# Memory attention's softmax: two scalings moved from VectorE to ScalarE, and wider spacing of its steps in a hybrid decoder step

## The chip, the cores and the metric

One core of one Trainium2 chip runs the whole program. The metric is the device time of one execution in microseconds (us); a kernel is run three times or more and the median is compared.

## The reference

One layer of a decoder trunk is computed for 1024 prompt tokens and 8 single-token samples, with a model width of 1024. From the normalised input one projection gives the operands of three branches: a stick-breaking attention (8 heads of 64, over the prompt, and over a paged cache of 2048 tokens for the samples), a short convolution, and a softmax cross-attention of 4 heads of 128 into 256 memory tokens. The branches are projected, gated and summed, and a feed-forward block of 4096 follows. The change lies in the cross-attention of the prompt:

```python
def cross_attn(q, mk, mv):
    s = jnp.einsum('bqhd,bmhd->bhqm', q.astype(jnp.float32), mk.astype(jnp.float32)) * (1.0 / math.sqrt(XA_HEAD_DIM))
    p = jax.nn.softmax(s, axis=-1)
    o = jnp.einsum('bhqm,bmhd->bqhd', p, mv.astype(jnp.float32)).astype(mv.dtype)
    return o.reshape(q.shape[0], q.shape[1], XA_WIDTH)
...
q, k, v, cb, cc, ch, xq = split_in(xn @ w_in[l])
y_sb = sb_prompt(q, k, v, b_sb[l])
...
y_xa = cross_attn(xq, mk, mv)
xp = merge_and_ffn(xp, xn, y_sb, y_conv, y_xa, *tail)
```

## The kernel before

Nearly all products are done in three matmuls (`mm3`, lines 149 to 152): each fp32 operand is split into a high and a low part, and high-high, high-low and low-high are added up in PSUM. The weights come in by DMA on the SP queue, ScalarE casts the high part (`wh`, line 126) and VectorE subtracts for the low part (`wl`, line 129). The stages follow each other: norms and memory keys and values; then one long stage in which the gemms of the input projection and of the gates run on TensorE (tile `g`, outputs of 128 channels by the chunks 384, 384 and 264 tokens) while three small jobs are woven in between them; then the merge, the output projection and the feed-forward block, which are dense matmuls.

The order of TensorE's instructions is fixed by the program's own planner, the class `Stream` (lines 165 to 236): it keeps a clock `S_.t`, adds the estimated cost of each matmul to it, and takes a step of a woven-in job when that clock passes the step's due time. Each job is a generator; `yield 7700.0` means "continue 7.7 us later by that clock", and `yield "f"` means "when the PSUM buffers `f` are free to use, at least 2.2 us after the last user". VectorE, ScalarE and the DMA queues execute in an order that the tile scheduler builds ahead of time; each engine works strictly through its own list, so an instruction that waits holds all that stand behind it. Steps under `high()` are placed early in that list, steps under `low()` fill the rest.

The three jobs are:

- `attention()` (line 666): the stick-breaking attention of the prompt. For each head pair and block of 128 queries: scores (tile `z`), a chain of ScalarE and VectorE passes that ends in `m` (lines 644 to 659), transposes into `wt` (line 709), a copy `th` (line 713) and the product `av` (line 727).
- `xattn()` (line 777): the memory attention, 4 heads by 4 blocks of 256 queries, 16 rounds. A round has three steps on TensorE, each `XA_NS` after the one before: the six score matmuls (`f<-mk,xq`), then four transposes of the weights (`f<-ident,pr`, line 811), then the six matmuls with the values (`f<-xth,mv` and `xtl`). Between the first and the second step stands the softmax: VectorE takes the maximum `mx` (line 799) and scales it (line 800), ScalarE does two exponentials with their sums (line 802), VectorE takes the reciprocal `sm` (line 804) and scales the weights `pr` (line 805).
- `decode()` (line 928): the samples. Pages of the key cache are multiplied and summed on VectorE (`kv` and `z` or `xs`, lines 937 and 938, low priority), and later pages of the value cache go through TensorE (line 891).

The softmax and the number that spaces the three steps:

```python
nc.vector.tensor_reduce(out=mx, in_=sc, axis=AX.X, op=ALU.max)
nc.vector.tensor_scalar(out=mx, in0=mx, scalar1=-XSC, scalar2=None, op0=ALU.mult)
...
nc.vector.reciprocal(out=sm, in_=sm)
nc.vector.tensor_tensor(out=pr, in0=pr, in1=sm.unsqueeze(2).to_broadcast([P, 2, 256]), op=ALU.mult)
yield XA_NS
yield "f"
...
XA_NS = 7700.0
```

Of the kernel before, what the change touches and what calls it, by code (L numbers as in the profile page):

```python
# [12 lines left out]
AF = mybir.ActivationFunctionType  # L13
ALU = mybir.AluOpType
# [4 lines left out]
P = 128  # L19
# [12 lines left out]
XSC = 128.0 ** -0.5  # L32
# [4 lines left out]
def body(ctx, tc, I, O):  # L37
    nc = tc.nc
# [85 lines left out]
    def split(hi, lo, src, scale=None, eng=None):  # L124
        if scale is None:
            cast = nc.scalar.copy(out=hi, in_=src)  # L126
            if first_exp:
                behind(cast, first_exp.pop())
            (eng or nc.vector).tensor_tensor(out=lo, in0=src, in1=hi.bitcast(F32), op=ALU.subtract)  # L129
        else:  # L130
            nc.scalar.mul(out=hi, in_=src, mul=scale)
            nc.vector.scalar_tensor_tensor(out=lo, in0=src, scalar=scale, in1=hi.bitcast(F32),
                                           op0=ALU.mult, op1=ALU.subtract)
# [15 lines left out]
    def mm3(ps, lh, ll, rh, rl, first, last):  # L149
        nc.tensor.matmul(out=ps, lhsT=lh, rhs=rh, start=first, stop=False)  # L150
        nc.tensor.matmul(out=ps, lhsT=lh, rhs=rl, start=False, stop=False)  # L151
        nc.tensor.matmul(out=ps, lhsT=ll, rhs=rh, start=False, stop=last)  # L152
# [87 lines left out]
    def cost(n):  # L240
        return 3 * n / 2.4
# [19 lines left out]
    def high():  # L261
        return tc.high_priority(offset=HIGH)
# [514 lines left out]
    def xattn():  # L777
        for h in range(4):
            yield f"x{h}p"
            yield 5000  # L780
            mk = cp.tile([P, 2, NMEM], F32R, name="mk", bufs=1)
            mv = cp.tile([P, 2, 2, P], F32R, name="mv", bufs=1)
            nc.sync.dma_start(out=mk.bitcast(F32), in_=mkscr[h])
            nc.sync.dma_start(out=mv.bitcast(F32), in_=mvscr[h])
            for q0 in range(0, S, 256):
                xq = cp.tile([P, 2, 256], F32R, name="xq", bufs=1)
                nc.sync.dma_start(out=xq.bitcast(F32), in_=xqs[h][:, :, q0:q0 + 256])
                yield XA_NS
                yield "f"
                sc = pf.tile([P, 2, 256], F32, name="f")  # L790
                for j in range(2):
                    qs = slice(j * P, (j + 1) * P)
                    mm3(sc[:, j], xq[:, 0, qs], xq[:, 1, qs], mk[:, 0], mk[:, 1], True, True)
                    S_.t += cost(256)
                mx = cp.tile([P, 2], F32, name="mx")
                sm = cp.tile([P, 2], F32, name="sm")
                pr = cp.tile([P, 2, 256], F32, name="pr", bufs=1)
                with high():
                    nc.vector.tensor_reduce(out=mx, in_=sc, axis=AX.X, op=ALU.max)
                    nc.vector.tensor_scalar(out=mx, in0=mx, scalar1=-XSC, scalar2=None, op0=ALU.mult)  # L800
                    for j in range(2):
                        nc.scalar.activation(out=pr[:, j], in_=sc[:, j], func=AF.Exp, scale=XSC, bias=mx[:, j:j + 1],
                                             accum_out=sm[:, j:j + 1])
                    nc.vector.reciprocal(out=sm, in_=sm)
                    nc.vector.tensor_tensor(out=pr, in0=pr, in1=sm.unsqueeze(2).to_broadcast([P, 2, 256]), op=ALU.mult)
                yield XA_NS
                yield "f"
                pt = pf.tile([P, 2, 256], F32, name="f")
                for t in range(2):
                    for j in range(2):  # L810
                        nc.tensor.transpose(out=pt[:, t, j * P:(j + 1) * P], in_=pr[:, j, t * P:(t + 1) * P],
                                            identity=ident)
                        S_.t += 109
                th = wk.tile([P, 2, 256], F32R, name="xth", tag="th", bufs=4)
                tl = wk.tile([P, 2, 256], F32R, name="xtl", tag="tl", bufs=1)
                with high():
                    split(th, tl, pt)
                yield XA_NS
                yield "f"
                av = pf.tile([P, 512], F32, name="f")[:, :256]  # L820
                for t in range(2):
                    mm3(av, mv[:, 0, t], mv[:, 1, t], th[:, t], tl[:, t], t == 0, t == 1)
                    S_.t += cost(256)
                yo = cp.tile([P, 256], F32, name="yo", bufs=1)
                with high():
                    nc.scalar.copy(out=yo, in_=av)
                nc.scalar.dma_start(out=yscr[8 + h][:, q0:q0 + 256], in_=yo)
        S_.done.add("xa")

    XA_NS = 7700.0  # L830


    z4 = z.rearrange("p g (b h) -> p g b h", h=8)
# [242 lines left out]
    for u in "qqqqkvkxxxxkvkcgcgcgcgcgcgcgcgcgcgcgcggggggggggggg":  # L1076
        n = count[u] = count.get(u, -1) + 1
        dict(q=add_q, k=add_k, v=add_v, x=add_x, c=add_c, g=add_g)[u](n)
    S_.spawn(attention())
    S_.spawn(xattn())  # L1080
    S_.spawn(decode())
    S_.run(lambda: {"att", "xa", "c32", "late3"} <= S_.done)
# [386 lines left out]
```

## Time and profile before

| | us |
|---|---|
| median of 3 runs | 1930.6 (1930.37 to 1934.13) |
| the profiled execution, its own time | 1933.35 |
| span of the profiled execution | 1931.5 |
| TensorE matmul busy in the span | 1845.9 |
| VectorE busy | 1115.0 |
| ScalarE busy | 801.2 |

The profile is of one execution. Its span runs from the first instruction to the last; 1.85 us of its own time lie outside. In the rows, PE is TensorE, DVE is VectorE, ACT is ScalarE, and SP issues DMAs. A row of a timeline has the start in us, the duration, the engine, the line and the operation, and in square brackets the idle time ahead of the instruction with what ended it. A stretch in a table of windows gives the busy time of each engine in it and the TensorE clock that was granted, 1.00 for the higher of its two levels (2.4 GHz) and 0.50 for the lower (1.2 GHz).

### The profile page before, as it was taken

How to read it: one execution, taken by the hardware profiler on the slowest of the kernel's cores; microseconds unless marked ns; L12 is line 12 of the kernel's file. 1: busy time of each engine (PE TensorE's matmuls, PEld its weight loads, DVE VectorE, ACT ScalarE, POOL GpSimd, SP SyncE). 2: the span in 40 equal slices, each digit the busy share in tenths (PEclk: the TensorE clock that was granted, in tenths of full speed). 3: DMA queues.
4: the chain of work that ended last, by engine and by line, in shares of the span. 5: the costliest groups of instructions: out<-in, count | busy, mean ns of one | idle time of the engine just before them, and what ended most of it. 6: DMA issues, size and time to landing. Idle time of an engine off the chain costs nothing.

```text
span 1931.5 us, 31789 instructions
## 1 busy us (share of the span) xinstructions
PE 1845.9 (96%) x12226; PEld 1734.4 (90%) x12226; DVE 1115.0 (58%) x1910; ACT 801.2 (41%) x1641; POOL 48.7 (3%) x54
## 2 busy tenths in 40 slices
PE   6999888999799999999999999999999999999996
PEld 5998777889788778778999999999999999999996
DVE  5337987899956555542347457254555555554437
ACT  6324555656666656652334445422211111222223
POOL 1000000000000000000031000000000000000003
PEclk9999999999899999999999999999999999999998
DMA  7558665555623556667554422211111111111122
GB/s 255 151 164 254 204 186 180 171 176 182 211 86 104 159 171 198 204 206 247 186 181 154 131 94 83 77 44 55 44 55 45 44 44 44 45 44 55 44 88 88
DMA packets 219464, 249.14 MB, mean 129 GB/s; under 512 B 14488, under 2 KB 162672, under 8 KB 219312
## 3 DMA queue, kind: packets, MB, share of 16 engines
q1 hardware_dynamic: 204080, 230.17, 38.1%
q10 hardware_dynamic: 15008, 16.90, 2.5%
q8 instruction: 96, 1.57, 0.3%
q14 instruction: 56, 0.46, 0.1%
q0 software_dynamic: 224, 0.04, 0.0%
HBM read 201.67 MB, written 45.40 MB: 128 GB/s over the span
## 4 chain that ended last, share of the span: by engine, by line
PE 82%; DVE 9%; DMA 3%; ACT 3%; issue 3%; SPq 0%; DVEq 0%; ACTq 0%
PE g L150 9%; PE g L152 8%; PE g L151 8%; PE u L150 8%; PE u L151 8%; PE u L152 8%; PE w L150 6%; PE w L151 6%; PE w L152 6%; PE m L150 2%; PE m L151 2%; PE m L152 2%; PE av L727 2%; PE z L628 2%; PE f L891 1%
## 5 line engine op out<-in xcount | busy, mean ns | idle before, releaser
L150 PE MATMUL g<-xh,wh 128*128 128x384 f32 (+1 forms) x1152 | 388.0, 337 | 3.8 <-DVE ql L129 3.8
L152 PE MATMUL g<-xh,wl 128*128 128x384 f32 (+1 forms) x1152 | 370.4, 321 | 1.9 <-DVE wl L129 1.9
L151 PE MATMUL g<-xl,wh 128*128 128x384 f32 (+1 forms) x1152 | 369.8, 321 | 0.0
L1347 DVE TENSOR_TENSOR facc<-w,facc 128x384 f32<-128x384 f32 (+3 forms) x336 | 171.5, 514 | 143.3 <-PE w L152 143.3
L150 PEld LDWEIGHTS g<-xh,wh 128*128 128x128 f32 x1152 | 220.6, 191 | 33.2 <-issue 26.9
L150 PE MATMUL w<-fh,dh 128*128 128x384 f32 (+3 forms) x720 | 232.6, 323 | 3.0 <-ACT facc L1345 2.5
L151 PE MATMUL w<-fl,dh 128*128 128x384 f32 (+3 forms) x720 | 231.3, 321 | 0.0
L152 PE MATMUL w<-fh,dl 128*128 128x384 f32 (+3 forms) x720 | 230.7, 320 | 0.0
L150 PE MATMUL u<-xh,wh 128*128 128x384 f32 (+1 forms) x720 | 229.3, 318 | 0.0
L152 PE MATMUL u<-xh,wl 128*128 128x384 f32 (+1 forms) x720 | 228.5, 317 | 0.0
L151 PE MATMUL u<-xl,wh 128*128 128x384 f32 (+1 forms) x720 | 228.4, 317 | 0.0
L152 PEld LDWEIGHTS g<-xh,wl 128*128 128x128 f32 x1152 | 219.6, 191 | 2.1 <-DVE wl L129 2.1
L151 PEld LDWEIGHTS g<-xl,wh 128*128 128x128 f32 x1152 | 220.6, 191 | 0.0
L129 DVE TENSOR_TENSOR wl<-wr,wh 128x1024 fp32r<-128x1024 f32 x104 | 127.3, 1224 | 115.7 <-ACT wh L126 115.4
L126 ACT CAST wh<-wr 128x1024 fp32r<-128x1024 f32 x104 | 109.0, 1048 | 106.7 <-PE g L151 44.9
L150 PEld LDWEIGHTS w<-fh,dh 128*128 128x128 f32 x720 | 136.5, 190 | 5.0 <-ACT facc L1345 2.8
L126 ACT CAST dh<-wr 128x1024 fp32r<-128x1024 f32 x32 | 33.5, 1050 | 256.4 <-PE w L151 239.6
L152 PEld LDWEIGHTS w<-fh,dl 128*128 128x128 f32 x720 | 136.4, 189 | 0.7
L151 PEld LDWEIGHTS w<-fl,dh 128*128 128x128 f32 x720 | 136.5, 190 | 0.6
L151 PEld LDWEIGHTS u<-xl,wh 128*128 128x128 f32 x720 | 135.4, 188 | 0.0
L150 PEld LDWEIGHTS u<-xh,wh 128*128 128x128 f32 x720 | 135.3, 188 | 0.0
L152 PEld LDWEIGHTS u<-xh,wl 128*128 128x128 f32 x720 | 135.2, 188 | 0.0
(293 smaller groups left out, 3393.0 us busy)
## 6 DMA issues: line engine op xcount, KB each, us to landing
kv<-in_cache_k_pages SPq DMA_DIRECT2D x128, 256.0 KB
kv<-in_cache_v_pages SPq DMA_DIRECT2D x96, 256.0 KB
wr<-in_w_up SPq DMA_DIRECT2D x32, 512.0 KB
wr<-in_w_down SPq DMA_DIRECT2D x32, 512.0 KB
wr<-in_w_in SPq DMA_DIRECT2D x28, 512.0 KB
lg<-lgscr SPq DMA_DIRECT2D x24, 516.0 KB
wr<-in_w_gate SPq DMA_DIRECT2D x24, 512.0 KB
lgscr<-lg ACTq DMA_DIRECT2D x48, 192.0 KB
```

The source lines that it names most:

```text
L126: cast = nc.scalar.copy(out=hi, in_=src)
L129: (eng or nc.vector).tensor_tensor(out=lo, in0=src, in1=hi.bitcast(F32), op=ALU.subtract)
L150: nc.tensor.matmul(out=ps, lhsT=lh, rhs=rh, start=first, stop=False)
L151: nc.tensor.matmul(out=ps, lhsT=lh, rhs=rl, start=False, stop=False)
L152: nc.tensor.matmul(out=ps, lhsT=ll, rhs=rh, start=False, stop=last)
L628: nc.tensor.matmul(out=zt[:, :w_], lhsT=hq[es], rhs=hk[es, k0:k1], start=True, stop=half != 0, tile_position=(64 * e, 0))
L727: nc.tensor.matmul(out=av[0][es], lhsT=hv[:, j, es], rhs=th[:, i, e], tile_position=(0, 64 * e), start=(r + n == R and k == 0), stop=(r == ...
L891: nc.tensor.matmul(out=ps[32 * j:32 * j + 32], lhsT=w[:, g, 32 * i:32 * i + 32], rhs=ts[j // 2][:, j % 2], start=True, stop=True, tile_pos ...
L1347: nc.vector.tensor_tensor(out=facc[:, n, cs], in0=ps, in1=facc[:, n, cs], op=ALU.add)
```

## The change

Three edits, all in `xattn()`. The scaling of the maximum by a constant goes to ScalarE. The scaling of the weights by the reciprocal sum goes to ScalarE, as two instructions of 256 columns where there was one of 512. The spacing of a round's three steps goes from 7.7 to 9.4 us of the planner's clock.

```diff
                     nc.vector.tensor_reduce(out=mx, in_=sc, axis=AX.X, op=ALU.max)
-                    nc.vector.tensor_scalar(out=mx, in0=mx, scalar1=-XSC, scalar2=None, op0=ALU.mult)
+                    nc.scalar.mul(out=mx, in_=mx, mul=-XSC)
                     for j in range(2):
                         nc.scalar.activation(out=pr[:, j], in_=sc[:, j], func=AF.Exp, scale=XSC, bias=mx[:, j:j + 1],
                                              accum_out=sm[:, j:j + 1])
                     nc.vector.reciprocal(out=sm, in_=sm)
-                    nc.vector.tensor_tensor(out=pr, in0=pr, in1=sm.unsqueeze(2).to_broadcast([P, 2, 256]), op=ALU.mult)
+                    for j in range(2):
+                        nc.scalar.activation(out=pr[:, j], in_=pr[:, j], func=AF.Copy, scale=sm[:, j:j + 1])
                 yield XA_NS
...
-    XA_NS = 7700.0
+    XA_NS = 9400.0
```

The number of matmuls stays as it is; 48 steps of the memory attention move later among them, and the scheduler builds the lists of the other engines anew. Lines behind 805 are one higher after the change.

VectorE's list in round 3 of the memory attention, before: from the scaling of the maximum (`mx`) to the scaling of the weights (`pr`). `kv` and `z` are the decode's page products, `u`, `a` and `m` the stick-breaking attention's.

```order
L800 TENSOR_SCALAR mx<-mx 128x2
L649 SCALAR_TENSOR_TENSOR u<-u,a 128x384
L651 TENSOR_TENSOR u<-m,u 128x384
L937 TENSOR_TENSOR kv<-kv,qb 128x1024
L651 TENSOR_TENSOR u<-m,u 128x384
L652 SCALAR_TENSOR_TENSOR a<-u,cy,a 128x384
L804 RECIPROCAL sm<-sm 128x2
L937 TENSOR_TENSOR kv<-kv,qb 128x1024
L938 TENSOR_REDUCE z<-kv 128x2x8
L652 SCALAR_TENSOR_TENSOR a<-u,cy,a 128x384
L658 TENSOR_TENSOR m<-m,a 128x384
L805 TENSOR_TENSOR pr<-pr,sm 128x512
```

The same place now: from the maximum to the reciprocal, which is VectorE's last part in the softmax.

```order
L799 TENSOR_REDUCE mx<-f 128x2
L939 TENSOR_REDUCE z<-kv 128x2x8
L129 TENSOR_TENSOR wl<-wr,wh 128x1024
L658 TENSOR_TENSOR m<-m,a 128x384
L938 TENSOR_TENSOR kv<-kv,qb 128x1024
L804 RECIPROCAL sm<-sm 128x2
```

Four other passes stand between the two, and none behind the reciprocal that the transposes need.

VectorE's list in round 8 now, behind the maximum (which stands just ahead of the first row) up to the reciprocal; `cv` is the convolution's, `xs` the decode's scores of memory tokens.

```order
L652 SCALAR_TENSOR_TENSOR a<-u,a 128x512
L938 TENSOR_TENSOR kv<-kv,qb 128x1024
L651 TENSOR_TENSOR u<-m,u 128x512
L938 TENSOR_TENSOR kv<-kv,qb 128x1024
L583 TENSOR_TENSOR cv<-g,cv 128x384
L656 COPY cy<-a 128x1
L658 TENSOR_TENSOR m<-m,a 128x512
L939 TENSOR_REDUCE xs<-kv 128x2x4
L652 SCALAR_TENSOR_TENSOR a<-u,a 128x512
L939 TENSOR_REDUCE xs<-kv 128x2x4
L583 TENSOR_TENSOR cv<-g,cv 128x264
L804 RECIPROCAL sm<-sm 128x2
```

This is the longest such piece of the 16 rounds; in rounds 1, 9, 10, 12 and 13 the reciprocal now stands right behind the maximum.

ScalarE's list in round 8 now, from the exponentials (`pr,sm`) to the two new scalings; `da`, `dd` and `w` are the decode's.

```order
L802 ACTIVATE pr,sm<-f,mx 128x256 x2
L986 ACTIVATE dd<-da 128x512
L645 ACTIVATE a<-m 128x512
L986 ACTIVATE dd<-da 128x512
L126 CAST wh<-wr 128x1024
L659 ACTIVATE m<-m 128x512
L645 ACTIVATE a<-m 128x512
L646 ACTIVATE a<-a 128x512
L713 COPY th<-wt 128x512
L806 ACTIVATE pr<-pr,sm 128x256 x2
L646 ACTIVATE a<-a 128x512
```

Eight passes of other jobs stand ahead of the scalings, and what stands behind them waits until the reciprocal is there.

## Rows read from the trace of the kernel before

**Rows 1.** Page, part 1: busy us, share of the span, instructions, by engine.

```profile
PE 1845.9 (96%) x12226; PEld 1734.4 (90%) x12226; DVE 1115.0 (58%) x1910; ACT 801.2 (41%) x1641; POOL 48.7 (3%) x54
```

**Rows 2.** Waits of PE: line, releaser, us in total, times, longest.

```profile
PE f L811 <- DVE pr L805: 30.5, 6, 8.3
...
PE wt L709 <- ACT m L659: 4.1, 4, 1.2
```

**Rows 3.** Timeline of PE: score matmuls of two rounds, and transposes that waited.

```profile
268.88 0.28 PE L152 MATMUL f<-mk,xq 128*128 128x256 f32 x1
...
284.86 1.09 PE L811 MATMUL f<-ident,pr 128*128 128x128 f32 x4 [6.86 <-DVE pr L805]
...
309.30 0.28 PE L152 MATMUL f<-mk,xq 128*128 128x256 f32 x1
...
326.53 1.09 PE L811 MATMUL f<-ident,pr 128*128 128x128 f32 x4 [7.84 <-DVE pr L805]
...
499.49 0.88 PE L811 MATMUL f<-ident,pr 128*128 128x128 f32 x3 [8.26 <-DVE pr L805]
...
533.38 1.08 PE L811 MATMUL f<-ident,pr 128*128 128x128 f32 x4 [4.26 <-DVE pr L805]
```

**Rows 4.** Windows behind the four longest waits: busy us by engine, then granted clock.

```profile
284.86:289.22 4.36, 4.36 (x21) 4.36 (x22) 3.19 (x4) 1.95 (x4) 0.00 (x0) 0.50 0.55 186
326.53:330.18 3.65, 3.65 (x16) 3.65 (x17) 3.65 (x4) 1.70 (x3) 0.00 (x0) 0.50 0.00 0
499.49:504.26 4.77, 4.77 (x22) 4.77 (x23) 4.77 (x8) 3.71 (x7) 0.00 (x0) 0.50 0.65 223
533.38:538.39 5.01, 5.01 (x28) 4.35 (x29) 0.94 (x3) 1.68 (x4) 0.00 (x0) 0.50 0.30 105
```

**Rows 5.** Timeline of DVE: round 3, and the maximum of rounds 4 and 5.

```profile
267.67 2.34 DVE L652 TENSOR_TENSOR_SCAN a<-u,a 128x512 f32<-128x512 f32 x2
...
272.83 0.69 DVE L799 TENSOR_REDUCE mx<-f 128x2 f32<-128x512 f32 x1
...
276.81 0.16 DVE L800 TENSOR_SCALAR mx<-mx 128x2 f32<-128x2 f32 x1
...
280.35 0.14 DVE L804 RECIPROCAL sm<-sm 128x2 f32<-128x2 f32 x1
280.41 1.20 DVE L937 TENSOR_TENSOR kv<-kv,qb 128x1024 f32<-128x1024 f32 x1
281.53 1.21 DVE L938 TENSOR_REDUCE z<-kv 128x16 f32<-128x1024 f32 x1
...
284.03 0.68 DVE L805 TENSOR_TENSOR pr<-pr,sm 128x512 f32<-128x512 f32 x1
...
313.99 0.67 DVE L799 TENSOR_REDUCE mx<-f 128x2 f32<-128x512 f32 x1
...
353.93 0.69 DVE L799 TENSOR_REDUCE mx<-f 128x2 f32<-128x512 f32 x1 [2.01 <-PE f L152]
```

**Rows 6.** Groups by line and form, 150 to 740 us: count, busy us, mean ns, idle.

```profile
L802 ACT ACTIVATE pr<-f,mx 128x256 f32<-128x256 f32 x32 | 14.9, 473 | 8.9 <-DVE mx L800 8.9
...
L557 ACT COPY qd<-g 128x8 f32<-128x8 f32 x4 | 0.7, 166 | 4.8 <-DVE ql L129 4.8
...
L129 DVE TENSOR_TENSOR xtl<-f,xth 128x512 fp32r<-128x512 f32 x16 | 10.9, 684 | 17.4 <-ACT xth L126 17.4
...
L805 DVE TENSOR_TENSOR pr<-pr,sm 128x512 f32<-128x512 f32 x16 | 10.9, 682 | 0.2
...
L800 DVE TENSOR_SCALAR mx<-mx 128x2 f32<-128x2 f32 x16 | 2.5, 159 | 0.2
```

**Rows 7.** Windows: length, busy us of PE, PEld, DVE, ACT, POOL; granted clock.

```profile
250.00:350.00 100.00, 84.99 (x622) 78.12 (x621) 76.95 (x103) 52.26 (x113) 0.00 (x0) 0.93 0.60 180
350.00:500.00 150.00, 134.73 (x902) 121.68 (x901) 137.58 (x194) 94.85 (x207) 0.20 (x2) 0.97 0.58 181
500.00:550.00 50.00, 45.74 (x317) 43.09 (x316) 35.83 (x56) 24.64 (x60) 0.00 (x0) 0.89 0.57 183
```

## Prediction, made before the changed kernel was run

> **What bounds the kernel now.** I read the page first, then the waits of TensorE, its timeline, and VectorE's timeline at the places found. TensorE's matmuls are busy for 96% of the span [rows 1], so the time can only fall where TensorE stands idle or runs at its lower clock. Of its waits one stands out: the transposes of the softmax weights wait for VectorE's scaling of them, 30.5 us in six waits, the longest 8.3 [rows 2]. Next on this stage is the attention's own chain, `wt` for `m`, with 4.1 us. The six waits fall in rounds 3, 4, 6, 7, 9 and 10; the four longest, 6.86, 7.84, 8.26 and 4.26 us, are shown [rows 3], and the other two are then 3.3 us together. Each of the four is followed by a stretch at a granted clock of 0.50, the lower of the two levels (1.2 GHz): 4.36, 3.65, 4.77 and 5.01 us, 17.8 us in all [rows 4]. TensorE had stood idle just before and was busy all through them, so half of that, 8.9 us, is lost too. The waits cost 30.5 + 8.9 = 39.4 us.
>
> Round 3 shows where they come from. The last score matmul ends at 268.88 + 0.28 = 269.16, and the transposes could have been issued at 284.86 - 6.86 = 278.00 [rows 3]: the room was 8.84 us (9.11 in round 4, by the same working). VectorE's steps lay at 272.83 (maximum), 276.81 (its scaling), 280.35 (reciprocal) and 284.03 (weights), done at 284.71 [rows 5]. The softmax's own work on VectorE is 0.69 + 0.16 + 0.14 + 0.68 = 1.67 us; the other 14 us it stands in line, behind decode products and the attention's passes. VectorE's list is what is late: from 350 to 500 us it is busy for 137.6 of 150 us [rows 7].
>
> **The change part by part.**
>
> *The weights' scaling leaves VectorE.* In round 3 four passes stood between the reciprocal and it, and cost 284.03 - 280.35 = 3.68 us with the reciprocal [rows 5]. Its place is taken by two ScalarE passes of 256 columns. The trace has no such copy; the nearest row, an exponential of the same width with a per-row operand, takes 0.473 us [rows 6]. Two take 0.95 us, against 0.68 on VectorE: 0.26 us dearer, and 0 to 0.95 us are the bounds of what it adds, as it may overlap. It also waits for what ScalarE has in hand, some 0.5 us.
>
> The Trainium skill speaks against this edit: "ScalarE: Activation LUTs", section "Rules for kernel authors", says to use VectorE for a multiplication. By its figures (186 ns + 0.833 ns a column, 93 ns more for a per-row operand) I estimate 0.49 us for each half, near the row's 0.473; the rule taken alone makes each round dearer, and it is a rival below. It prices the instruction and not the line that it stands in.
>
> *The maximum's scaling leaves VectorE.* 276.81 - 272.83 = 3.98 us passed between the two in round 3 [rows 5], of which 0.69 are the maximum itself. On ScalarE it costs about 0.17 us (the copy of 8 columns, 0.166 [rows 6]); the bounds are 0 and 0.47. Ahead of it stand up to two passes that ScalarE may do in the meantime.
>
> *The spacing* adds 9.4 - 7.7 = 1.7 us, so the room grows from 8.8 to about 10.5 us. TensorE does the same matmuls in another order, so this costs no matmul time. The last round's end moves by 48 steps x 1.7 = 82 us, to about 810 us; the attention itself ends later, and the merge needs the results only after the gates. I cost this at nothing; the cover is the remaining gemms of the gates.
>
> *What is left of the waits.* Per round: VectorE's arrears when the scores are done, the maximum, the passes to the reciprocal, the reciprocal, and ScalarE's 1.45 us (0.95 + 0.5). The arrears were 272.83 - 269.16 = 3.7 us in round 3, 313.99 - 309.58 = 4.4 in round 4, and nothing in round 5, where VectorE waited [rows 3, 5]; I take 2.5, about their mean. The pieces of the new order are priced start to start by rows 5: 1.12 us for a product or a sum of 1024 columns (281.53 - 280.41), 1.17 for a scan of 512, 0.61 for a pass of 512. Round 3: 2.5 + 0.69 + 3.8 + 0.14 + 1.45 = 8.6, inside 10.5. Round 8 is the longest: four products and sums 4.5, two scans 2.3, two passes 1.2, the rest (two narrower passes and a copy) 0.8, together 8.8; with 2.5 + 0.69 + 0.14 + 1.45 it takes 13.6 us, and there the waits do not vanish: some 3.1 us, or 5.0 with arrears of 4.4. With the lower clock behind a wait of that size (half of 5.01 [rows 4]) it is 5.6 us. The other rounds fit, with at most 1 to 2 us over at full arrears.
>
> *What is late next.* If TensorE no longer stands still, VectorE has less time for the same work. From 350 to 500 us it does 137.6 us. The change takes 0.68 + 0.16 = 0.84 us per round from it in the four rounds that will lie there (3.4 us), and moves one of five rounds out (0.84 removed anyway, and the maximum, the reciprocal and the 0.68 of `xtl` [rows 6], 2.4 us in all): 131.8 remain. At the share it reaches today (137.6/150 = 0.917) that needs 143.7 us, so this stretch shrinks by 6.3 us and not by the 13.9 that its waits are worth (30.5 - 6.86 - 7.84 - 4.26 = 11.5, and 4.77/2 = 2.4). That gives back 7.6 us, and round 8 lies inside it, so its 5.6 are not counted twice. From 250 to 350 us TensorE's work at full clock is 85.0 - 4.0 = 81.0 us; VectorE has 77.0 - 1.7 = 75.3, which at 0.917 take 82.1: 1 us given back. From 500 to 550 us VectorE has slack (35.8 of 50).
>
> *ScalarE's new line.* 16 x (0.17 + 0.95) = 18 us more work on an engine that is busy for 94.9 of 150 us at its fullest [rows 7], so most is covered. What stands behind a scaling that waits for the reciprocal (casts of weights, `th`, releases of PSUM) is held. No row shows that; between nothing and 16 x 0.95 = 15 us, I take 5, as ScalarE idles for a third of the time. A gain below nothing would be the 4.1 us of `wt` waits that a new order may shed.
>
> **The sum**: 39.4 - 7.6 - 1 - 5 = 25.8 us. The profiled execution took 1933.35 us, so 1907.5; it is 2.75 us above the median of the three runs, so against the median the number is 1930.6 - 25.8 = **1904.8 us**. A measurement of this kernel can tell about 0.2%, 3.9 us, from no change.
>
> **The rivals.**
>
> *All of it comes back.* VectorE lifts its share, since its own idle times wait on TensorE. 1930.6 - 39.4 = 1891 us. For it: VectorE stands idle at the maximum of round 5 for 2.01 us only because TensorE is late [rows 5]. Against it: round 8's order.
>
> *VectorE becomes the bound.* Of 300 us from 250 to 550 it works 250.4 [rows 7]; if its 49.6 us of idle time stay (they wait on ScalarE's chain, not on TensorE), only its saved work comes back: eight rounds x 0.84 and 2.4 for one moved out, 9 us: 1921.6 us, and new waits of `wt` on `m` or of `g` on `wl`. For it: 92% busy in the middle stretch. Against: 77% and 72% on either side.
>
> *The edit is dearer and nothing else counts.* The rule above, as a mechanism here: if the arrears and not the order set the end, each of the six waits only grows by 0.26 us, 1.6 us, and 16 rounds at most 4: 1932 us, no change. Against it: the room alone must shorten six waits by up to 1.7 us each.
>
> *ScalarE's list stands (slower).* Each scaling holds the list until the reciprocal is there. In round 8 ScalarE has about eight passes, some 5 us, to cover 8.8 us of VectorE, and stands for about 3.5. If all 16 rounds stood so long, and the weight casts and `th` behind them held TensorE, that is 56 us against the 39.4 recovered: 1947 us. It decides from 39.4/16 = 2.5 us a round. Against it: in five rounds the reciprocal now follows the maximum directly, and elsewhere the passes between take half of round 8's.
>
> That the change does not do what it says is excluded by the order: the passes behind the reciprocal are gone, and the steps have moved.
>
> **How the numbers follow.** The forecast (give-back of 4 to 20 us, 1895 to 1911) has 0.52, all back 0.10, VectorE the bound (1912 to 1926) 0.20, no change 0.08, slower 0.10. Faster by over 0.2% is 0.52 + 0.10 + 0.20 = 0.82. The range goes from 1889, just under the case in which all comes back, to 1926, and leaves out no change and slower, 0.18.
>
> **What would show it.** The waits of TensorE on the softmax weights, now from ScalarE at line 806, should fall from 30.5 us to under 8, with the largest in round 8 near 460 us; the clock should be 1.00 in nearly all of 250 to 550 us; VectorE's maximum-to-reciprocal time in round 3 should be about 4.5 us and not 7.5. VectorE's share from 350 us on should stay near 0.92. The prediction is wrong if other waits of TensorE in this stage (`wt` on `m`, `g` on `wl`, evacuations by ScalarE) grow to over 15 us, or if those on line 806 stay above 15.

## The result, and the profile after

The change took 1893.8 us (median of 4 runs, 1890.7 to 1895.5) against 1931.0 us for the kernel before (4 runs, 1930.4 to 1934.1): a ratio of 0.9815, 95% interval 0.9802 to 0.9828, or 37 us less. The profiled execution took 1894.98 us, its span is 1893.2 us.

The page of the changed kernel, part 1:

```profile
span 1893.2 us, 31801 instructions
...
PE 1834.7 (97%) x12226; PEld 1723.4 (91%) x12226; DVE 1104.3 (58%) x1878; ACT 812.0 (43%) x1689; POOL 48.7 (3%) x54
```

TensorE executes as many matmuls as before [rows 1] and is busy for 1845.9 - 1834.7 = 11.2 us less: that is time at the lower clock which is gone. Added up over the stretches at a granted clock of 0.50, it was busy for 40.8 us before and for 17.1 now, and half of that difference is 11.8. Its idle time fell from 1931.5 - 1845.9 = 85.6 to 1893.2 - 1834.7 = 58.5 us, by 27.1. Together this is the 38.3 us by which the span is shorter.

The waits of TensorE in the changed kernel, from 150 to 960 us (line, releaser, total, times, longest):

```profile
PE wt L709 <- ACT m L659: 4.2, 3, 2.4
PE f L450 <- ACT qd L557: 4.1, 3, 2.1
PE g L150 <- DVE cx L579: 2.5, 1, 2.5
...
PE f L812 <- ACT pr L806: 1.0, 1, 1.0
```

The 30.5 us for the softmax weights [rows 2] have become 1.0. What the attention's chain costs (`wt` for `m`) is as before, 4.2 against 4.1.

Round 3 in the changed kernel. Its last score matmul on TensorE:

```profile
280.89 0.28 PE L152 MATMUL f<-mk,xq 128*128 128x256 f32 x1
```

And the timeline of VectorE:

```profile
284.80 0.69 DVE L799 TENSOR_REDUCE mx<-f 128x2 f32<-128x512 f32 x1
...
289.26 0.16 DVE L804 RECIPROCAL sm<-sm 128x2 f32<-128x2 f32 x1
```

From the maximum to the reciprocal it is 4.46 us now, where it was 280.35 - 272.83 = 7.5 [rows 5]. The scores ended at 281.17, 3.6 us before the maximum, so VectorE's arrears were what they had been (3.7); what shrank is what stands between.

Round 8 in the changed kernel, the one round whose transposes still wait by more than 0.1 us. The last score matmul on TensorE:

```profile
469.63 0.28 PE L152 MATMUL f<-mk,xq 128*128 128x256 f32 x1
```

VectorE's two parts of the softmax:

```profile
472.19 0.67 DVE L799 TENSOR_REDUCE mx<-f 128x2 f32<-128x512 f32 x1
...
481.62 0.14 DVE L804 RECIPROCAL sm<-sm 128x2 f32<-128x2 f32 x1
```

ScalarE's scaling of the maximum, the pass ahead of the weights' scalings, and these:

```profile
474.39 0.19 ACT L800 ACTIVATE mx<-mx 128x2 f32<-128x2 f32 x1
...
481.64 0.58 ACT L713 COPY th<-wt 128x512 f32<-128x512 f32 x1
482.11 0.92 ACT L806 ACTIVATE pr<-pr,sm 128x256 f32<-128x256 f32 x2
```

And the transposes on TensorE:

```profile
482.68 0.95 PE L812 MATMUL f<-ident,pr 128*128 128x128 f32 x4 [0.96 <-ACT pr L806]
```

The arrears were 472.19 - 469.91 = 2.3 us, maximum to reciprocal 9.4, and ScalarE was busy with other passes right up to the scalings: they began 0.35 us after the reciprocal was done (482.11 against 481.76). TensorE was there at 481.72, 11.8 us behind the scores, and could begin when the first half was scaled.

The windows that answer to [rows 7]:

```profile
250.00:350.00 100.00, 96.07 (x727) 87.25 (x726) 86.57 (x115) 59.99 (x137) 0.00 (x0) 1.00 0.67 207
350.00:500.00 150.00, 143.09 (x957) 130.20 (x956) 141.81 (x193) 103.04 (x219) 0.20 (x2) 0.98 0.60 185
500.00:550.00 50.00, 49.95 (x352) 45.40 (x351) 36.48 (x57) 32.93 (x80) 0.00 (x0) 1.00 0.48 150
```

TensorE gained in all three stretches. VectorE's share rose too: to 0.87 from 0.77, to 0.945 from 0.917, and a little in the third.

### The profile page after: what moved, and what is told of

Read it like the earlier page. It is cut to its first block, busy times and chain, and to the rows that moved or that the text cites. A ratio compares the mean times of both kernels' runs of the same rounds, so it can differ in the third digit from the quotient of the medians.

```text
span 1893.2 us, 31801 instructions
## 1 busy us (share of the span) xinstructions
PE 1834.7 (97%) x12226; PEld 1723.4 (91%) x12226; DVE 1104.3 (58%) x1878; ACT 812.0 (43%) x1689; POOL 48.7 (3%) x54
## 4 chain that ended last, share of the span: by engine, by line
PE 83%; DVE 8%; DMA 4%; issue 3%; ACT 2%; SPq 0%; DVEq 0%; ACTq 0%
PE g L150 9%; PE g L152 8%; PE g L151 8%; PE u L150 8%; PE u L151 8%; PE u L152 8%; PE w L150 6%; PE w L151 6%; PE w L152 6%; PE m L150 2%; PE m L151 2%; PE m L152 2%; PE f L892 2%; PE av L727 2%; PE z L628 2%
```

## The experiments

Two theories stood at the start. Theory L (list): the softmax stands in VectorE's list behind other work, and the scalings on ScalarE take it out of there. Theory R (room): the room between a round's steps decides, and not the engine. A diff is against the changed kernel unless the text says otherwise. In the sections below TensorE's order is that of the kernel before wherever the spacing is 7.7, and that of the change wherever it is 9.4, but for the run of the late rows, which moves some transposes. The tile scheduler builds the lists of the other engines anew for each kernel, so two kernels differ in them by more than the edit. A ratio is always to the kernel before on the same chip; its interval stands behind it.

### Scalings on ScalarE without the spacing

```diff
-    XA_NS = 9400.0
+    XA_NS = 7700.0
```

> Both scalings on ScalarE, spacing left at 7.7, so TensorE's order is that of before. Theory L (the softmax stands in VectorE's list, the scalings on ScalarE take it out): the passes between maximum and reciprocal come to 3.9, 3.4, 4.4 and 5.3 us in rounds 3, 4, 9 and 10, so with 2.5 us of arrears the chain is 8 to 10 us against a room of 8.8; 2 to 6 us of waits on the weights stay, time 1896 to 1903. Theory R (the room between the steps decides, the engine does not): 20 us or more of the 30.5 stay, time 1915 or above.

Measured: 1904.1 us, ratio 0.9863 (0.9843 to 0.9882), about 26 us gained. Its waits of TensorE, 150 to 900 us:

```profile
PE g L152 <- DVE wl L129: 5.1, 2, 3.0
PE wt L709 <- ACT m L659: 4.7, 2, 3.5
...
PE f L812 <- ACT pr L806: 4.0, 3, 3.3
```

The waits on the weights are what theory L said (4.0 us); the time is 1 us above its bounds. Waits on `wl` of 5.1 us have come up beside them, which the kernel before did not have in this stretch. The 20 us or more of theory R did not come.

### Spacing without the scalings

```diff
-    XA_NS = 7700.0
+    XA_NS = 9400.0
```

(on the kernel before)

> Scalings on VectorE, spacing 9.4, so TensorE's order is that of the change. Theory L: VectorE's list has 13.7 us of passes between maximum and weights in round 2, 9.4 in round 5, 7.0 in round 6 and 14.8 in round 8, more than the room of 10.5 (14 in round 2) takes; waits of about 16 us stay, the largest (8 to 9 us) in round 8, with some 5 us at the lower clock, time 1908 to 1918. Theory R: the room alone does it, waits under 6 us, time 1892 to 1898.

Measured: 1903.5 us, ratio 0.9862 (0.9844 to 0.9881). Its waits on the weights, and the largest of them in the timeline of TensorE:

```profile
PE f L811 <- DVE cv L596: 5.5, 1, 5.5
...
PE f L811 <- DVE pr L805: 2.7, 2, 1.7
```

```profile
487.00 1.09 PE L811 MATMUL f<-ident,pr 128*128 128x128 f32 x4 [5.52 <-DVE cv L596]
```

8.2 us of waits stay, half of what theory L had and more than R's; the largest is in round 8, where L had it. The time lies between the bounds of the two theories. So the room by itself takes away three quarters of the waits. By the ratios either part alone gains about 26 us, and both together 36: they cut the same waits.

### Which of the two scalings

Only the weights on ScalarE, spacing 7.7:

```diff
+                    nc.vector.tensor_scalar(out=mx, in0=mx, scalar1=-XSC, scalar2=None, op0=ALU.mult)
-                    nc.scalar.mul(out=mx, in_=mx, mul=-XSC)
...
-    XA_NS = 9400.0
+    XA_NS = 7700.0
```

> Only the scaling of the weights on ScalarE, spacing 7.7. Theory L: the passes up to the reciprocal stay as before (7.0, 6.4, 7.3 and 6.4 us in rounds 3, 4, 9 and 10), those behind it are gone; some 11 us of waits stay, time 1902 to 1910. Theory R: 1915 or above.

Only the maximum on ScalarE, spacing 7.7:

```diff
+                    nc.vector.tensor_tensor(out=pr, in0=pr, in1=sm.unsqueeze(2).to_broadcast([P, 2, 256]), op=ALU.mult)
-                    for j in range(2):
-                        nc.scalar.activation(out=pr[:, j], in_=pr[:, j], func=AF.Copy, scale=sm[:, j:j + 1])
...
-    XA_NS = 9400.0
+    XA_NS = 7700.0
```

> Only the scaling of the maximum on ScalarE, spacing 7.7. Theory L: maximum to reciprocal falls to 3.9, 3.4, 4.4 and 3.3 us in rounds 3, 4, 9 and 10, but 2.1 to 3.9 us of passes stand behind the reciprocal; some 7 us of waits stay, time 1898 to 1908. Theory R: 1915 or above.

Measured: 1920.0 us for the weights alone, ratio 0.9952 (0.9934 to 0.9969), and 1911.0 us for the maximum alone, ratio 0.9898 (0.9879 to 0.9917). Waits on the weights with the weights' scaling alone:

```profile
PE f L812 <- ACT pr L806: 14.9, 4, 5.0
```

and with the maximum's alone (the second row is put down to a ScalarE pass, but these transposes, too, began 0.14 us after VectorE had scaled their weights):

```profile
PE f L811 <- DVE pr L805: 11.5, 5, 4.0
...
PE f L811 <- ACT da L983: 3.7, 1, 3.7
```

Both are slower than expected: about 15 us of waits stay in each, against 11 and 7 expected, so theory L's way of adding up a chain from the list is too kind by a few us. The time with the weights alone lies where theory R had it (1915 or above), the waits do not (20 us or more). In time the tiny instruction on two columns is worth twice the one on 512.

The same two with the spacing of 9.4. The maximum alone:

```diff
+                    nc.vector.tensor_tensor(out=pr, in0=pr, in1=sm.unsqueeze(2).to_broadcast([P, 2, 256]), op=ALU.mult)
-                    for j in range(2):
-                        nc.scalar.activation(out=pr[:, j], in_=pr[:, j], func=AF.Copy, scale=sm[:, j:j + 1])
```

> The change with the scaling of the weights put back on VectorE: maximum on ScalarE, spacing 9.4. Theory L: VectorE's list holds 3.7, 1.1, 2.6, 2.9 and 4.4 us of passes behind the reciprocal in rounds 2, 5, 6, 7 and 8, and in round 8 10.0 us in all, about as much as the room: 3 to 6 us of waits, nearly all in round 8, 3 to 8 us slower than the change. If the scaling of the weights on ScalarE is what counts beside the room: as slow as spacing alone, some 10 us above the change.

The weights alone:

```diff
+                    nc.vector.tensor_scalar(out=mx, in0=mx, scalar1=-XSC, scalar2=None, op0=ALU.mult)
-                    nc.scalar.mul(out=mx, in_=mx, mul=-XSC)
```

> The change with the scaling of the maximum put back on VectorE: weights on ScalarE, spacing 9.4; with it every combination of the three edits is measured. Theory L: the maximum's scaling keeps its place in VectorE's list, which has 9.6, 7.1 and 12.0 us of passes between maximum and reciprocal in rounds 2, 5 and 8; about 7 us of waits in round 8 and 1 to 2 in round 5, with 3 us at the lower clock: 8 to 13 us slower than the change, about as slow as spacing alone. If either scaling on ScalarE does as well as the other beside the spacing: within 4 us of the change.

Measured: 1891.9 us with the maximum, ratio 0.9799 (0.9775 to 0.9823); 1901.0 us with the weights, ratio 0.9853 (0.9834 to 0.9872). Waits on the weights with the maximum's scaling on ScalarE:

```profile
PE f L811 <- DVE pr L805: 2.1, 1, 2.1
```

and with the weights':

```profile
PE f L812 <- ACT pr L806: 4.1, 1, 4.1
```

The weights' run came out near what was expected: 7 us slower than the change (8 to 13 expected) and as slow as the spacing alone, with its one wait in round 8, of 4.1 us and not 7. The maximum's did not: 3 to 8 us more than the change and nearly all of the waits in round 8 were expected. It was no slower, and its one wait is in round 6. Its list had changed as well: in round 8 six passes stand between the maximum and the reciprocal, where the change has eleven, so the two kernels differ in more than the place of the scaling.

All eight combinations, as ratios to the kernel before:

| on ScalarE | spacing 7.7 | spacing 9.4 |
|---|---|---|
| neither | 1 | 0.9862 |
| weights | 0.9952 | 0.9853 |
| maximum | 0.9898 | 0.9799 |
| both | 0.9863 | 0.9815 |

Beside the spacing, the weights' scaling on ScalarE gains nothing that can be measured (0.9862 to 0.9853, and 0.9799 to 0.9815 with the maximum there); the maximum's gains 0.4 to 0.6%. The version without the weights' edit is as fast as the change; their intervals overlap.

### The same softmax with a lighter VectorE

The kernel before, in which the decode's 72 page products work on 16 of 1024 columns and their sum is a copy of 16 columns (of 8 for the memory tokens): the samples' scores leave out the rest.

```diff
-                    p = nc.vector.tensor_tensor(out=t, in0=t, in1=qb.unsqueeze(1).to_broadcast([P, 2, 512]), op=ALU.mult)
-                    s = nc.vector.tensor_reduce(out=out, in_=t.rearrange("p g (h d) -> p g h d", d=d), axis=AX.X, op=ALU.add)
+                    p = nc.vector.tensor_tensor(out=t[:, :, 0:8], in0=t[:, :, 0:8], in1=qb[:, 0:8].unsqueeze(1).to_broadcast([P, 2, 8]), op=ALU.mult)
+                    s = nc.vector.tensor_copy(out=out, in_=t[:, :, 0:512 // d])
```

> The kernel before (scalings on VectorE, spacing 7.7), but each of the decode's 72 page products on VectorE works on 16 of its 1024 columns and its sum is a copy of 16 columns, so the samples' scores leave out the rest: about 72 x 2.2 = 158 us less of VectorE. Theory L: with the decode's passes short, VectorE's list holds the softmax up no more; waits on the weights under 4 us, time 1885 to 1895 with the softmax as before. Theory R, and the theory that the softmax's own steps are too slow on VectorE: 20 us or more of waits stay, time above 1912.

Measured: 1880.9 us, ratio 0.9750 (0.9734 to 0.9767). All waits of TensorE from 150 to 960 us, and the fullest stretch:

```profile
PE wt L709 <- ACT th L713: 4.4, 2, 4.3
PE f L450 <- ACT qd L557: 3.5, 3, 1.7
PE m L150 <- DVE macc L1180: 3.0, 1, 3.0
PE f L604 <- DVE va L901: 1.9, 1, 1.9
PE g L150 <- ACT vf L516: 0.4, 1, 0.4
```

```profile
350.00:500.00 150.00, 145.75 (x1018) 135.15 (x1017) 91.63 (x208) 100.16 (x223) 0.10 (x1) 0.99 0.66 203
```

Softmax, engines and spacing are those of the kernel before, and yet not one wait on the weights is left once VectorE has 92 in place of 138 us to do in that stretch. The other work in VectorE's list made the waits, not the softmax's own steps. Theory R by itself, and the theory that the softmax's own steps are too slow on VectorE, are refuted. The time is 4 us below the bounds of theory L.

### ScalarE's line

```diff
+                    jk = cp.tile([P, 256], F32, name="jk", bufs=1)
+                    for j in range(2):
+                        nc.scalar.activation(out=jk, in_=pr[:, j], func=AF.Copy, scale=sm[:, j:j + 1])
                     for j in range(2):
                         nc.scalar.activation(out=pr[:, j], in_=pr[:, j], func=AF.Copy, scale=sm[:, j:j + 1])
```

> The change, with the two scalings of the weights done twice (first into a scratch tile): about 1.0 us more on ScalarE in each of 16 rounds, on the path to the transposes and ahead of what stands behind them. If ScalarE's list stands (the 5 us of the prediction's sum, 0.95 us a round, reach TensorE): 8 to 20 us slower than the change. If the room covers it: within 4 us of the change.

Measured: 1901.2 us, ratio 0.9856 (0.9840 to 0.9873), so about 8 us slower than the change when the two ratios are compared. Its waits on the weights:

```profile
PE f L815 <- ACT pr L809: 8.2, 5, 3.8
```

One scaling takes 0.51 us in the changed kernel (median of 32), so 32 more are 16 us on ScalarE, and half of them reach the end; the waits on the weights alone are 7.2 us longer than in the change. The time lies at the lower edge of the first case (8 to 20 us slower) and is not within the second: the path by way of ScalarE has little to spare.

### More room

```diff
-    XA_NS = 9400.0
+    XA_NS = 11500.0
```

> The change with a spacing of 11.5 in place of 9.4. The change's own wait on the weights is 1.0 us, so by theory L there is nothing left to gain by room: within 4 us of the change, up or down, by the new order alone. By theory R more room frees more: 5 us or more faster than the change.

Measured: 1906.3 us, ratio 0.9879 (0.9862 to 0.9895), 12 us slower than the change, which neither theory had. TensorE's timeline at the end of the stage, and the window there:

```profile
899.92 0.95 PE L812 MATMUL f<-ident,pr 128*128 128x128 f32 x4 [1.55 <-ACT pr L806]
902.11 0.58 PE L150 MATMUL f<-xth,mv 128*128 128x256 f32 x1 [1.24 <-ACT xth L126]
...
908.78 0.69 PE L150 MATMUL m<-yh,wh 128*128 128x384 f32 x1 [4.23 <-ACT yh L126]
```

```profile
870.00:925.00 55.00, 45.67 (x272) 41.68 (x271) 15.85 (x19) 22.85 (x32) 0.00 (x0) 0.88 0.50 164
```

The last round ends right ahead of the merge (`m<-yh`), with no gemm of the gates left to lie beside it: 9.3 us idle, and a clock of 0.88 on average. That is the cover which the prediction named for the later rounds, used up. Up to there hardly anything was lost: the last gemm of the gates ends at 898.4 us in this run and at 898.5 in the change, where the merge follows without a gap. To tell this from harm by the spacing itself:

```diff
-    XA_NS = 9400.0
+    XA_NS = 10200.0
```

> The change with a spacing of 10.2, so the last round ends 48 x 0.8 = 38 us later than in the change, some 70 us ahead of the merge (with 11.5 it ended just ahead of the merge, and the merge waited). If the loss at 11.5 came from that end alone, and the room is enough already: within 4 us of the change. If wider spacing harms in itself: 4 us or more slower.

Measured: 1893.0 us, ratio 0.9802 (0.9777 to 0.9827), no different from the change. So the loss at 11.5 came from the end.

### The waits that are left

```diff
-                S_.at(2500, lambda: S_.when("f", lambda: rows_out(qd, qscr[1, :, P * h:P * h + P])))
+                S_.at(5500, lambda: S_.when("f", lambda: rows_out(qd, qscr[1, :, P * h:P * h + P])))
```

> The change, with the transposes of the samples' memory queries (line 450) placed 5.5 in place of 2.5 us of the planner's clock behind their gemm. They wait 6.0 us in the change (4.1 for ScalarE's copy, 1.9 for a store). If these waits cost what they show: 4 to 7 us faster than the change. If the stage is held by VectorE's list there, other waits take their place: within 3 us.

Measured: 1894.9 us, ratio 0.9823 (0.9805 to 0.9842), no different from the change. Its waits of TensorE, 150 to 960 us:

```profile
PE wt L709 <- ACT m L659: 10.9, 5, 3.2
```

No wait on line 450 is left where 6.0 us had been (2.3 us for the same copy now stand on `g`), and the attention's chain waits for 10.9 where it was 4.2: other waits took the place of most of them. All waits of this stretch come to 18.9 us, against 21.9 in the change.

Taking work from VectorE by another road: the subtraction for the low part of 26 weight tiles on GpSimd (the expectation counted about 20).

```diff
-        add_gemm(f"x{i}p", wview(w_in, 3072 + i * P, P), xproj(i))
+        add_gemm(f"x{i}p", wview(w_in, 3072 + i * P, P), xproj(i), eng=nc.gpsimd)
...
-        add_gemm(f"gate{t}", wview(w_gate, t * P, P), gates(t))
+        add_gemm(f"gate{t}", wview(w_gate, t * P, P), gates(t), eng=nc.gpsimd if t < 8 else None)
```

(the convolution's weights and the last two of `k` likewise)

> The change, with the subtraction for the low part of about 20 weight tiles (line 129, 1.2 us each on VectorE) done on GpSimd, some 24 us less for VectorE between 200 and 560 us. If VectorE's list still holds TensorE there (the remaining waits of wt, g and f are some 20 us between 150 and 560 us): 5 to 12 us faster than the change. If GpSimd's subtraction, 2.4 us by the nearest row, comes too late or slows VectorE: waits of g on wl of over 5 us, no gain or a loss.

Measured: 1914.4 us, ratio 0.9907 (0.9872 to 0.9942), 18 to 21 us slower than the change. VectorE's timeline, then GpSimd's:

```profile
308.14 1.22 DVE L938 TENSOR_TENSOR kv<-kv,qb 128x1024 f32<-128x1024 f32 x1
309.28 1.22 DVE L652 TENSOR_TENSOR_SCAN a<-u,a 128x512 f32<-128x512 f32 x1
310.41 3.35 DVE L938 TENSOR_TENSOR kv<-kv,qb 128x1024 f32<-128x1024 f32 x1
```

```profile
309.24 3.44 POOL L129 TENSOR_TENSOR wl<-wr,wh 128x1024 fp32r<-128x1024 f32 x1 [14.38 <-PE wt L709]
```

A product that takes 1.22 us took 3.35 when it began beside a GpSimd subtraction, and ended 1.1 us after that had ended. The subtraction took 1.1 us more than the shortest of the 26 (2.36 us), and a scan of VectorE had begun at nearly the same time (309.28 against 309.24). Over 150 to 560 us the products average 1340 ns in place of 1213 and GpSimd's subtractions 2829, so the engines held each other up. VectorE gained nothing by it: 26 instructions of 1.2 us had left its list, and it was busy for 1108.0 us where it is 1104.3 in the change. The Trainium skill has a rule for this ("SBUF — State Buffer", section "SBUF: two separate sides"): a VectorE instruction with two SBUF inputs and a GpSimd instruction that reads SBUF share a pair of ports; the one that starts first holds it for its whole length, and the other is blocked. These rows agree, if the scan had the ports first, the subtraction then, and the product last.

TensorE's idle time is 11.0 us longer than in the change and its busy time 9.1. None of its waits from 150 to 960 us is put down to `wl`, the sign that had been named; those on ScalarE's `qd` grew from 4.1 to 9.3 us. That the shared ports make up the whole loss is not shown.

## Why the prediction was right, and where its sum was off

The direction and the cause held: the time went where the prediction had put it, into the transposes that waited for VectorE's list, and the lower clock behind them. The time, 1893.8 us, lies inside the range and 11 us below the forecast. It is below the band of the forecast itself (1895 to 1911) and next to the rival in which all of the waits come back (1891 us), which had a chance of 0.10.

*The waits.* 39.4 us were named as removable. The waits on the weights fell by 29.5 us, other waits of TensorE from 150 to 960 us rose by 4 (16.9 to 20.9, added up over their rows), and the lower clock cost 11.2 us less where 8.9 had been priced. That the 38.3 us of the span come so near to the 39.4 is in part luck. From 250 to 550 us, where the price was set, TensorE was busy at the lower clock for 20.9 us before and 6.2 now, which is worth 7.4 us: the four stretches are gone, and two short ones came up near 350 and 367 us. The rest, some 4 us, lies past 900 us, in stretches near 941, 1231 and 1900 us of the kernel before; nothing here ties those to the softmax. The waits that were named as a sign of being wrong (`wt` on `m`, `g` on `wl`, evacuations by ScalarE) stayed under 15 us: 4.2, 1.4 and 4.8.

*Round 8.* It was named as the one round that keeps a wait, and is. The chain was priced at 13.6 us and took 13.1 to the end of the second scaling (469.91 to 483.03). The wait was 0.96 and not 3.1 us, because TensorE needed 11.8 us and not 10.5 to come there, and the first of the four transposes needs only the first half. It came at 482 us and not near 460.

*What is late next: the step that failed.* VectorE's share of 0.917 was taken as the most it can reach, and 7.6 + 1 us were given back for it. It reached 0.945 in that stretch, 0.964 with the spacing of 10.2, and 0.87 in the stretch ahead. Such a share is no ceiling where part of the engine's idle time is a wait for the very engine that it holds up: the largest single idle time that VectorE had in that stretch of the kernel before was a wait for TensorE's scores, 2.0 us [rows 5], and the idle times there that a matmul ended fell from 5.3 to 1.9 us. This is the mechanism of the rival that all comes back. The limit is real, though, only further off: with the decode's work lightened the kernel before ran 13 us faster than the change, and in the changed kernel a wait that was moved away came back as another.

*ScalarE's new line: 5 us priced, hardly any to be seen.* The waits of TensorE that are put down to ScalarE, from 150 to 960 us, went from 8.5 to 10.0 us, and 1.0 of that is the softmax weights. In round 8, where ScalarE was to stand for about 3.5 us, its exponentials began only at 476.67 us, and its timeline shows no idle time from there to the scalings. The margin is thin: in the run with the weights scaled twice about half of 16 us more reached the end.

*The rivals.* VectorE as the bound, the dearer edit and the standing ScalarE list did not come. As to the rule of the Trainium skill ("ScalarE: Activation LUTs", section "Rules for kernel authors"), each half took 0.51 us, near the 0.49 estimated from the page's figures (section "What ACT_TABLE_LOAD costs"). The two are dearer than the one of 0.68 us on VectorE, and that is not what counted. But the combinations give the rule some right: beside the spacing, the weights' scaling gains nothing measurable by its move. The prediction had not parted the two scalings. Why the maximum's is worth more, with about the same waits on the weights left in the two kernels at 7.7, is only argued: it lets the exponentials, the sums and the reciprocal all come earlier, and stands for 0.2 us in ScalarE's list, not 1.0. The traces show no single wait that holds the difference. With the weights' scaling on ScalarE in place of the maximum's, TensorE's idle time is 2.2 us longer at 7.7 and 5.8 us longer at 9.4, and its busy time 2.4 and 3.8 us; the waits on the attention's `m`, a ScalarE pass, are 5.3 against 3.4 us and 6.7 against 4.0. The cause stays open.

## What to carry to other kernels

Where an engine works through a fixed list, look at where an instruction of a short chain stands in it, not at what it costs: a step of 0.16 us in the middle of a chain was worth twice one of 0.68 us at its end, though why is not settled here. A wait like this can be cut by taking the chain out of the full list or by giving its consumer more to do first; the two cut the same waits, so their gains don't add, and room runs out when the work that covers the tail does. A busy share of 92% was not a ceiling here, as part of the idle rest was waiting for the very engine that was being freed.

## What was not expected of the hardware

GpSimd next to VectorE was the largest surprise: 26 subtractions on GpSimd, meant to relieve VectorE, stretched a product of VectorE from 1.22 to 3.35 us where they met, left VectorE as busy as it had been, and came with a time 18 to 21 us longer. And the lower clock makes up 11.2 us of the 38.3 by which the span fell, nearly a third, of which about 7.4 lie in the stretch of the waits that were removed.
